# Key search and gates of a product-key layer, queued on VectorE behind the low parts of their own pair of blocks

## The chip, the cores and the metric

The kernel runs on one core of a Trainium2 chip. The metric is the time of one execution on the device in microseconds (us); of several runs the median is given. A profile is one execution, recorded by the hardware profiler; its span reaches from the first to the last instruction.

## The reference

Two transformer blocks on 256 tokens of width 1024, in float32. The first has two layers (stick-breaking attention and retention as mixers, each followed by a mixture of experts), the second runs a state space branch beside a sparse attention, and then a layer of 16384 experts that are picked by product keys. The change lies in that last layer:

```python
def peer_ffn(x, w_q, sub_k1, sub_k2, u_tab, v_tab):
    ...
    s1 = jnp.einsum('bshd,hnd->bshn', q[..., 0, :], sub_k1.astype(f32))
    s2 = jnp.einsum('bshd,hnd->bshn', q[..., 1, :], sub_k2.astype(f32))
    v1, i1 = lax.top_k(s1, PEER_TOPK)
    v2, i2 = lax.top_k(s2, PEER_TOPK)
    cand_s = (v1[..., :, None] + v2[..., None, :]).reshape(...)
    top_s, pos = lax.top_k(cand_s, PEER_TOPK)
    experts = jnp.take_along_axis(cand_i, pos, axis=-1)
    gates = jax.nn.softmax(top_s, axis=-1)
    ...
        act = jax.nn.gelu(jnp.einsum('ced,cd->ce', u, xc.astype(f32))) * gc
        return jnp.einsum('ce,ced->cd', act, v_tab[ec].astype(f32))
```

Each token has 8 heads; a head scores 128 keys of each of two halves, takes the 16 best of both, and of their 256 sums the 16 best. That gives 128 experts a token, each with a gate.

## The kernel before

The kernel does not gather experts. It computes U times every token for all 16384 experts, in a pass over 128 blocks of U (128 experts, 1024 wide, 512 KB each), keeps the result in `big` (key 2 on partitions, key 1, token), multiplies it by gates, which are zero for experts that a token did not pick, and then makes a second pass over 128 blocks of V.

**The pass over U** (`peer`, L1467) takes the blocks in pairs. SP loads a block (L1478, tile `raw`, three buffers). ScalarE rounds it to float32r (L1480, the cast, tile `pair`, three buffers). What the rounding left, the low part, is subtracted in two shares at L1483: VectorE takes three of the eight chunks (UD = 3), GpSimd the other five. TensorE then does 24 matmuls for the block (L162, `ps<-hn,pair`). After a pair ScalarE applies the gelu (L1489 for tokens whose gates are there already, L1492 for the others), and VectorE multiplies the former by their gates (L1490).

**The side work** is a generator, `select` (L1365), that yields pieces with a cost. For each half t of the tokens it searches the keys, head by head, and then runs `gates` (L1427). A head's search is L1382 to L1406: the best 16 of both score rows by MAX8, FIND_INDEX8 and MATCH_REPLACE8 (L1382, L1383, L1385, four, four and two a head), the 256 sums (L1389), their best 16 (L1393 to L1396), the places decoded (L1397 to L1399), and the keys looked up with a one-hot (L1403 on VectorE, L1405 on GpSimd, L1406 on VectorE). The softmax over the gates follows once for a half (L1409 to L1414, the exponential on ScalarE at L1410), and a transposition on TensorE (L186). `gates` then works in groups of four tokens: VectorE builds one-hots (L1440 to L1443, tile `s`), TensorE multiplies them (L162, `y<-s`, eight matmuls a group), and the result goes into `big`: where blocks of U have come, VectorE multiplies (L1454), for the others ScalarE copies (L1456).

`spend` (L114) emits pieces until their cost has used up what a call gives: 4.16 after each head of the scores before the pass, PACE = 2.81 after each pair of blocks in it. A head's search costs 5.5 in four pieces, a group of gates 1.8.

```python
    def spend(self, more):
        self.credit += more
        while self.credit > 0 and self.side:
            self.credit -= next(self.side, 1e9)
```

**What sets the order.** Each engine executes its instructions in one fixed order. A scheduler makes it when the program is built: it steps through a modelled time, and at each step gives an engine the instruction that was emitted earliest among those that are ready in that model. Pieces of the search read the scores alone, which are there before the pass begins; so nothing but the place of emission ties them to a pair of blocks. In the order before, the search of the second half stands on VectorE between blocks 9 and 42 of the pass, among the gates of the first half, though its pieces are emitted after pairs from block 52 on.

Of the kernel before, what the change touches and what calls it, by code (L numbers as in the profile page):

```python
# [50 lines left out]
# the order in which the pieces of the state space branch, of the attention and of the gates are emitted  # L51
# [3 lines left out]
class Net:  # L55
# [49 lines left out]
    def background(self, n=1):  # L105
        """emits n pieces of the work that has only to be done some time"""
        while n and self.jobs:
            try:
                next(self.jobs[0])
                n -= 1  # L110
            except StopIteration:
                self.jobs.pop(0)

    def spend(self, more):  # L114
        """emits pieces of the work of self.side, which yields what each costs, at `more` a call"""
# [31 lines left out]
    def split(self, hi, lo, src, eng=None):  # L147
        """hi = src in float32r, lo = the rest; eng, in short pieces, for lo"""
# [22 lines left out]
    def warm(self, src, n=1):  # L171
        """products that nobody reads, once src is there: they keep the clock of the tensor engine up while it waits"""
# [32 lines left out]
    def ada_rows(self, i, j, slot, out):  # L205
        """silu(c) @ w of a third (shift, scale, gate): rows 32c.. of out hold columns 256c.. of the third"""
# [22 lines left out]
    def ada_all(self, i, j, first):  # L229
        """emits in pieces; leaves self.mod[i, j] = scale, shift columns and gate rows"""  # L230
# [8 lines left out]
    def ada_cols(self, m, g_b, i, j):  # L239
        """scale and shift as columns [P, KB], folded with the last norm's g and b"""  # L240
# [24 lines left out]
    def gate_row(self, m2):  # L265
        """1 + gate on every partition [P, D]"""
# [9 lines left out]
    def row(self, cols):  # L276
        """columns [P, KB] as a row of D on every partition"""
# [10 lines left out]
    def ln_rows(self, i, j):  # L288
        """what the norm after a sublayer needs: 1 + gate, g and b on every partition"""
# [13 lines left out]
    def layer_norm(self, x, y, i, j):  # L303
        """x: residual [P, T, D], replaced by the new one; y: psum tiles y[t][half]; returns xhat"""
# [36 lines left out]
    def transposed(self, src, each, scales=None):  # L341
        """src [P, T, D], or its rows times the diagonals of scales -> each(k, psum [P, S]) for the KB blocks of D"""
# [1452 lines left out]
```

## Time and profile before

| | |
|---|---|
| median of 3 runs | 2150.25 us (2148.62 to 2151.22) |
| span of the profiled execution | 2146.3 us; its time outside the span is not recorded |
| TensorE (PE) busy | 1998.3 us, 93% |
| VectorE (DVE) busy | 1244.3 us, 58% |
| ScalarE (ACT) busy | 787.7 us, 37% |
| GpSimd (POOL) busy | 489.9 us, 23% |
| pass over U on TensorE | 1316 to 1782 us |

The profile gives a span and busy times within it; a run's time also counts what lies around the span. A busy share is a mean over stages with different limits, so the pass over U is read by itself, in stretches. The granted clock (PEclk) is TensorE's, 1.00 for 2.4 GHz, 0.50 for 1.2 GHz, and values between are means over a stretch.

### The profile page before, as it was taken

How to read it: one execution, taken by the hardware profiler on the slowest of the kernel's cores; microseconds unless marked ns; L12 is line 12 of the kernel's file. 1: busy time of each engine (PE TensorE's matmuls, PEld its weight loads, DVE VectorE, ACT ScalarE, POOL GpSimd, SP SyncE). 2: the span in 40 equal slices, each digit the busy share in tenths (PEclk: the TensorE clock that was granted, in tenths of full speed). 3: DMA queues.
4: the chain of work that ended last, by engine and by line, in shares of the span. 5: the costliest groups of instructions: out<-in, count | busy, mean ns of one | idle time of the engine just before them, and what ended most of it. 6: DMA issues, size and time to landing. Idle time of an engine off the chain costs nothing.

```text
span 2146.3 us, 32368 instructions
## 1 busy us (share of the span) xinstructions
PE 1998.3 (93%) x12822; PEld 1567.6 (73%) x12823; DVE 1244.3 (58%) x2474; ACT 787.7 (37%) x1224; POOL 489.9 (23%) x349
## 2 busy tenths in 40 slices
PE   6999999969999899997877999988999999999998
PEld 4967544428998744545765889888999998888886
DVE  4555111146885411115798569999627995565565
ACT  3353111124454111114323543444444444444444
POOL 1002000022331200002354144544665550000000
PEclk9999999989999899998998999999999999999999
DMA  9797799985875699994232361334454445555554
GB/s 389 287 398 275 286 395 394 392 317 213 297 277 171 235 387 391 395 395 180 109 106 90 123 234 40 128 119 138 165 184 158 143 148 186 188 193 188 189 192 149
DMA packets 155599, 496.11 MB, mean 231 GB/s; under 512 B 10144, under 2 KB 10560, under 8 KB 146864
## 3 DMA queue, kind: packets, MB, share of 16 engines
q1 hardware_dynamic: 152592, 483.42, 62.5%
q0 software_dynamic: 2848, 10.53, 1.3%
q8 instruction: 104, 1.70, 0.3%
q14 instruction: 55, 0.45, 0.1%
HBM read 486.30 MB, written 7.61 MB: 230 GB/s over the span
## 4 chain that ended last, share of the span: by engine, by line
PE 47%; DVE 14%; issue 2%; ACT 1%; POOL 1%; POOLq 0%; ACTq 0%; DVEq 0%
PE ps L162 25%; PE y L162 21%; DVE pair L1483 1%; DVE t L1134 1%; DVE hl L152 1%; DVE et L1406 1%; DVE i L1383 1%; DVE s L1440 1%; DVE t L1135 1%; DVE pos L1394 0%; DVE s L1442 0%; DVE v L1382 0%; POOL hl L159 0%; DVE t L1129 0%; DVE t L1130 0%
## 5 line engine op out<-in xcount | busy, mean ns | idle before, releaser
L162 PE MATMUL ps<-hn,pair 128*128 128x256 f32 x3072 | 394.8, 289 | 6.5 <-DVE pair L1483 6.5
L162 PEld LDWEIGHTS ps<-hn,pair 128*128 128x128 f32 x3072 | 382.5, 195 | 7.6 <-DVE pair L1483 7.5
L1483 POOL TENSOR_TENSOR pair<-raw,pair 128x640 fp32r<-128x640 f32 x128 | 241.7, 1892 | 183.6 <-ACT pair L1480 161.8
L162 PE MATMUL ps<-w,t 128*64 128x512 f32 x576 | 256.0, 598 | 10.6 <-ACT t L734 4.1
L162 PE MATMUL ps<-hl,t 128*64 128x512 f32 x576 | 255.6, 599 | 0.0
L150 ACT CAST hl<-w 128x2048 fp32r<-128x2048 f32 x79 | 150.1, 1903 | 146.5 <-PE ps L162 80.5
L152 DVE TENSOR_TENSOR pair<-raw,pair 128x1024 fp32r<-128x1024 f32 x128 | 156.8, 1225 | 67.2 <-ACT pair L150 67.2
L162 PE MATMUL y<-pair,tmp 128*128 128x512 f32 x768 | 189.5, 396 | 0.0
L162 PE MATMUL y<-pair,eT 128*128 128x512 f32 x768 | 186.3, 392 | 0.0
L162 PEld LDWEIGHTS y<-pair,tmp 128*128 128x128 f32 x768 | 144.7, 188 | 33.6
L162 PEld LDWEIGHTS y<-pair,eT 128*128 128x128 f32 x768 | 144.3, 188 | 32.2
L162 PEld LDWEIGHTS ps<-w,t 128*64 128x64 f32 x576 | 76.8, 137 | 124.5 <-issue 112.3
L152 DVE TENSOR_TENSOR hl<-w,hl 128x2048 fp32r<-128x2048 f32 x54 | 127.4, 2361 | 55.5 <-ACT hl L150 52.0
L1480 ACT CAST pair<-raw 128x1024 fp32r<-128x1024 f32 x128 | 134.5, 1053 | 50.7 <-PE ps L162 43.0
L159 POOL TENSOR_TENSOR hl<-w,hl 128x512 fp32r<-128x512 f32 x52 | 75.7, 1486 | 301.5 <-ACT hl L150 297.3
L688 DVE TENSOR_TENSOR t<-t,ps 128x512 f32<-128x512 f32 x16 | 11.0, 687 | 213.4 <-PE ps L162 213.4
L150 ACT CAST pair<-raw 128x1024 fp32r<-128x1024 f32 x128 | 133.8, 1045 | 1.1 <-issue 1.1
L162 PE MATMUL ps<-hl,a 128*128 128x256 f32 x1008 | 130.3, 287 | 1.8 <-ACT hl L150 1.8
L162 PEld LDWEIGHTS ps<-hl,a 128*128 128x128 f32 x1008 | 124.0, 191 | 6.1 <-issue 2.1
L1483 DVE TENSOR_TENSOR pair<-raw,pair 128x384 fp32r<-128x384 f32 x128 | 91.3, 715 | 43.5 <-ACT pair L1480 43.5
L162 PEld LDWEIGHTS ps<-a,hl 128*128 128x128 f32 x864 | 106.3, 195 | 4.2 <-issue 2.9
L162 PE MATMUL ps<-a,hl 128*128 128x256 f32 x864 | 108.5, 288 | 0.7 <-DVE a L152 0.5
(422 smaller groups left out, 3067.3 us busy)
## 6 DMA issues: line engine op xcount, KB each, us to landing
raw<-peer_u SPq DMA_DIRECT2D x128, 512.0 KB, 3.4
raw<-peer_v SPq DMA_DIRECT2D x128, 512.0 KB, 4.2
w<-ada_w SPq DMA_DIRECT2D x35, 1024.0 KB, 8.7
w<-moe_w_gate SPq DMA_DIRECT2D x24, 1024.0 KB, 16.0
w<-moe_w_up SPq DMA_DIRECT2D x24, 1024.0 KB, 14.1
w<-moe_w_down SPq DMA_DIRECT2D x24, 1024.0 KB, 14.1
hl<-moe_w_gate SPq DMA_DIRECT2D x24, 1024.0 KB, 14.3
hl<-moe_w_up SPq DMA_DIRECT2D x24, 1024.0 KB, 14.2
```

Of the source, the lines that this page charges most:

```text
L150: nc.scalar.copy(hi, src)
L152: nc.vector.tensor_tensor(lo, src, hi.bitcast(F32), op=OP.subtract)
L159: eng.tensor_tensor(lo[:, q], src[:, q], hi.bitcast(F32)[:, q], op=OP.subtract)
L162: self.nc.tensor.matmul(out, lhsT=lhsT, rhs=rhs, start=start, stop=stop, skip_group_check=True)
L688: nc.vector.tensor_tensor(hid, hid, pu, op=OP.mult)
L1134: V.tensor_tensor_scan(w[:, ri], d, a[:, ri], 0.0, op0=OP.mult, op1=OP.add)
L1135: V.tensor_tensor(a, w, bc(c), op=OP.mult)
L1383: V.max_index(ix[:, a, rs], v[:, a, rs], s)
L1406: V.tensor_reduce(et[:, 0:2, h], oh.rearrange("p a k j -> p a j k"), axis=AX.X, op=OP.add)
L1440: V.tensor_tensor(ol, self.iota4, of(0), op=OP.is_equal)
L1480: nc.scalar.copy(up[:, 0], ur)
L1483: eng.tensor_tensor(up[:, 1, ks], ur[:, ks], up[:, 0, ks].bitcast(F32), op=OP.subtract)
```

## The change

`issue_after(ins)` adds to each instruction that its block emits on the engine of `ins` an edge behind `ins`, in the order alone: no semaphore, no wait. `at` is VectorE's share of the low part of the pair's second block. So the pieces that `spend` emits after a pair stand on VectorE behind that low part. Instructions of the pieces on other engines get no edge. The test for an empty share went too (both shares are nonempty), and comments were dropped, with their lines kept; from L1483 on lines shift by one, and the low part's own line is L1482 in the changed kernel.

```diff
                 for eng, ks in ((V, slice(0, UD)), (nc.gpsimd, slice(UD, KB))):
-                    if ks.start < ks.stop:
-                        eng.tensor_tensor(up[:, 1, ks], ur[:, ks], up[:, 0, ks].bitcast(F32), op=OP.subtract)
+                    lo = eng.tensor_tensor(up[:, 1, ks], ur[:, ks], up[:, 0, ks].bitcast(F32), op=OP.subtract)
+                    at = lo if eng is V else at
...
             self.ready = i + 2
-            self.spend(PACE)
+            with self.tc.issue_after(at.ins):
+                self.spend(PACE)
```

What becomes of the order, at three places. Names in the rows: `pair` is the block's tile with its low part, `raw` the block as loaded; `s<-c_iota` and `s<-s,eT` are one-hots of the gates; `v`, `i`, `pos`, `cand`, `fi`, `oh`, `et` belong to the search.

VectorE in the pass over U, from the low part of block 26 to that of block 27 in the kernel before:

```order
L1483 TENSOR_TENSOR pair<-raw,pair 128x384
L1394 MAX_INDEX pos<-top,cand 128x8
L1454 TENSOR_TENSOR big<-y,big 128x4x24
L1490 TENSOR_TENSOR big<-s,big 128x2x40
L1440 TENSOR_TENSOR s<-c_iota_9783,eT 128x512
L1443 TENSOR_TENSOR s<-c_iota_9783,eT 128x512
L1442 TENSOR_TENSOR s<-s,eT 128x512
L1406 TENSOR_REDUCE et<-oh 128x2x16
L1387 CAST fi<-i_13294 128x32
L1396 MATCH_REPLACE cand<-top,cand 128x256
L1441 TENSOR_TENSOR s<-s,eT 128x512
L1483 TENSOR_TENSOR pair<-raw,pair 128x384
```

and, in the changed kernel, from the low part of block 25 to that of block 27, a whole pair:

```order
L1482 TENSOR_TENSOR pair<-raw,pair 128x384
L1490 TENSOR_TENSOR big<-s,big 128x2x40
L1440 TENSOR_TENSOR s<-c_iota_9783,eT 128x512
L1443 TENSOR_TENSOR s<-c_iota_9783,eT 128x512
L1454 TENSOR_TENSOR big<-y,big 128x4x24
L1441 TENSOR_TENSOR s<-s,eT 128x512
L1482 TENSOR_TENSOR pair<-raw,pair 128x384
L1442 TENSOR_TENSOR s<-s,eT 128x512
L1482 TENSOR_TENSOR pair<-raw,pair 128x384
```

The search (L1394, L1406, L1387, L1396) has left this place; a pair now has its two low parts, one product L1490, and gates alone.

VectorE further on, from block 59 to block 64, where the order before has this and nothing else:

```order
L1483 TENSOR_TENSOR pair<-raw,pair 128x384 x2
L1490 TENSOR_TENSOR big<-tmp,big 128x2x128
L1483 TENSOR_TENSOR pair<-raw,pair 128x384 x2
L1490 TENSOR_TENSOR big<-s,big 128x2x128
L1483 TENSOR_TENSOR pair<-raw,pair 128x384 x2
```

In the changed kernel, from the low part of block 61 to just ahead of that of block 62:

```order
L1482 TENSOR_TENSOR pair<-raw,pair 128x384
L1394 MAX_INDEX pos<-top,cand 128x8
L1382 MAX v_13136<-s 128x8
L1397 TENSOR_SCALAR pos<-pos 128x16
L1398 TENSOR_SCALAR pos<-pos 128x16
L1383 MAX_INDEX i_13137<-v_13136,s 128x8
L1399 CAST fi<-pos 128x32
L1385 MATCH_REPLACE s<-v_13136,s 128x128
L1403 TENSOR_TENSOR oh<-c_iota_9784,fi 128x512
L1382 MAX v_13136<-s 128x8
L1490 TENSOR_TENSOR big<-s,big 128x2x128
L1383 MAX_INDEX i_13137<-v_13136,s 128x8
```

Half a head's search now stands between two low parts here, and the rest of the head within four blocks; the eight heads of the second half take blocks 53 to 83.

ScalarE at blocks 82 and 83, before:

```order
L1480 CAST pair<-raw 128x1024 x2
L1489 ACTIVATE tmp<-ps 128x2x128
L1492 ACTIVATE big<-ps 128x2x128
L1480 CAST pair<-raw 128x1024 x2
L1489 ACTIVATE s<-ps 128x2x128
L1492 ACTIVATE big<-ps 128x2x128
L1480 CAST pair<-raw 128x1024 x2
```

and in the changed kernel:

```order
L1480 CAST pair<-raw 128x1024 x2
L1410 ACT_TABLE_LOAD
L1410 ACTIVATE et<-et 128x128
L1489 ACT_TABLE_LOAD
L1489 ACTIVATE s<-ps 128x2x128
L1492 ACTIVATE big<-ps 128x2x128
L1480 CAST pair<-raw 128x1024 x2
```

The exponential of the second half's softmax with its two table loads came from block 41 to just ahead of the cast of block 82. GpSimd's L1405 moved with the search, one to four low parts, and the load of the residual that GpSimd issues moved from ahead of its low part of block 38 to that of block 80. SP's order is unchanged, and so is VectorE's from block 86 on.

## Rows read from the trace of the kernel before

**Rows 1.** the page: span and busy time of engines (us, share of the span, instructions).
```profile
span 2146.3 us, 32368 instructions
...
PE 1998.3 (93%) x12822; PEld 1567.6 (73%) x12823; DVE 1244.3 (58%) x2474; ACT 787.7 (37%) x1224; POOL 489.9 (23%) x349
```

**Rows 2.** the page: busy tenths in 40 slices of the span, 53.7 us each.
```profile
PE   6999999969999899997877999988999999999998
...
DVE  4555111146885411115798569999627995565565
```

**Rows 3.** windows of stretches that begin at blocks 3, 12, 42, 52, 84 of U.
```profile
core 0: us, PE busy (x) PEld busy (x) DVE busy (x) ACT busy (x) POOL busy (x), PEclk, DMA share, GB/s
1325.60:1361.15 35.55, 31.17 (x238) 30.69 (x236) 35.33 (x114) 15.92 (x19) 20.73 (x14) 0.90 0.47 148
1361.15:1496.97 135.82, 116.90 (x907) 112.29 (x905) 134.35 (x376) 57.88 (x83) 61.51 (x39) 0.95 0.36 121
1496.97:1532.42 35.45, 35.45 (x299) 35.11 (x297) 31.73 (x53) 18.75 (x31) 19.16 (x11) 1.00 0.48 162
1532.42:1624.97 92.55, 92.55 (x774) 92.55 (x772) 29.02 (x56) 42.30 (x63) 61.56 (x32) 1.00 0.54 177
1624.97:1782.40 157.43, 157.43 (x1315) 155.53 (x1314) 137.60 (x226) 68.27 (x121) 84.76 (x43) 1.00 0.46 151
```

**Rows 4.** waits of TensorE, blocks 12 to 41: total us, times, longest.
```profile
PE y L162 <- DVE s L1442: 9.5, 10, 1.8
PE y L162 <- DVE s L1441: 6.6, 7, 1.5
PE ps L162 <- DVE pair L1483: 2.8, 4, 2.1
```

**Rows 5.** waits of ScalarE, the same stretch.
```profile
ACT big L1456 <- DVE big L1454: 63.7, 21, 6.9
```

**Rows 6.** waits of TensorE, blocks 3 to 11.
```profile
PE ps L162 <- DVE pair L1483: 3.6, 1, 3.6
PE y L186 <- DVE et L1406: 0.7, 1, 0.7
```

**Rows 7.** windows of VectorE (us, busy, clock, DMA), search beside low parts.
```profile
1316.00:1346.00 30.00, 29.71 (x122) 0.89 0.29 91
```

**Rows 8.** groups of instructions on VectorE, 1316 to 1346 us.
```profile
L1483 DVE TENSOR_TENSOR pair<-raw,pair 128x384 fp32r<-128x384 f32 x6 | 4.4, 735 | 0.2 <-ACT pair L1480 0.2
...
L1382 DVE MAX8 v<-s 128x8 f32<-128x128 f32 x14 | 3.5, 275 | 0.0
```

**Rows 9.** groups on VectorE and GpSimd, blocks 52 to 83.
```profile
L1483 DVE TENSOR_TENSOR pair<-raw,pair 128x384 fp32r<-128x384 f32 x31 | 17.3, 558 | 39.2 <-ACT pair L1480 39.2
...
L1490 DVE TENSOR_TENSOR big<-tmp,big 128x256 f32<-128x256 f32 x8 | 3.4, 424 | 11.3 <-ACT tmp L1489 11.3
...
L1483 POOL TENSOR_TENSOR pair<-raw,pair 128x640 fp32r<-128x640 f32 x32 | 61.7, 1929 | 31.4 <-ACT pair L1480 31.4
```

**Rows 10.** timeline of VectorE, L1397 twice: start, us taken.
```profile
1342.06 0.15 DVE L1397 TENSOR_SCALAR pos<-pos 128x16 uint32<-128x16 uint32 x1
...
1430.94 1.57 DVE L1397 TENSOR_SCALAR pos<-pos 128x16 uint32<-128x16 uint32 x1
```

**Rows 11.** the instructions of L1405 on GpSimd: duration min/median/max in ns.
```profile
L1405 POOL TENSOR_TENSOR oh<-oh,fi x16: 1047/1052/1639, 1289.9 to 1487.5; 128x512 f16<-128x512 f16 x16
```

**Rows 12.** timeline of ScalarE around the softmax of the first half.
```profile
1342.54 1.28 ACT L1410 ACT_TABLE_LOAD   x1
1343.83 0.31 ACT L1410 ACTIVATE et<-et 128x128 f32<-128x128 f32 x1
...
1345.10 1.28 ACT L1492 ACT_TABLE_LOAD   x1
```

**Rows 13.** the page: the costliest groups, the cast of a block of U.
```profile
L1480 ACT CAST pair<-raw 128x1024 fp32r<-128x1024 f32 x128 | 134.5, 1053 | 50.7 <-PE ps L162 43.0
```

## The prediction

> **What bounds the kernel now.** I read the busy times first: TensorE works in 93% of the span, VectorE in 58% [rows 1]. So TensorE sets the time, and anything that makes it wait counts. Next the slices [rows 2], each 53.7 us: TensorE falls to 7 and 8 in slices 25 to 28 (1288 to 1502 us), just where VectorE stands at 9 four times running; then VectorE drops to 6 and 2 while TensorE is at 9. The same engine is too full and then nearly empty, within one pass over U.
>
> I then cut this pass by blocks of U, at the starts of blocks 3, 12, 42, 52 and 84 on TensorE [rows 3]. In the fourth stretch (blocks 52 to 83) TensorE never waits: 774 matmuls in 92.55 us, 0.1196 us each. That is the floor. At it, the second stretch (blocks 12 to 41) would need 907 x 0.1196 = 108.5 us; it takes 135.8, so 27.3 us are lost. The first loses 35.55 - 238 x 0.1196 = 7.1 us. The third (299 matmuls) and the fifth (1315) come out within 0.4 us of the floor. VectorE is busy for 134.35 of 135.82 us in the second stretch and for 29.02 of 92.55 in the fourth.
>
> What ends TensorE's waits in the second stretch [rows 4]: 16.1 us for one-hots of the gates (L1441, L1442), 2.8 for low parts. Those one-hots are cheap; they are late since key search for the second half of the tokens, which depends on no block of U, stands among them on VectorE. Idle adds up to 18.9 us; the other 8.4 of the 27.3 are matmuls that run at a lower granted clock after the gaps (0.95 in this stretch, 1.00 in the three behind it).
>
> **The change, part by part.** No arithmetic, tile or transfer is added; only the order differs. In the changed order blocks 12 to 51 have gates and low parts alone on VectorE, the eight heads of search for the second half stand in blocks 53 to 83, and from block 86 on VectorE's order is the old one.
>
> 1. *Blocks 12 to 41, search gone.* The nearest row is the third stretch of the old kernel: blocks 42 to 51, the same gates of the first half with low parts and no search, in nearly the order that blocks 12 to 41 now get. It runs at the floor, at 31.73 us of VectorE in 35.45 [rows 3]. What ScalarE does there is a little different: it copies the part of the gates whose block has not come yet, and that part is larger early on. Those copies now wait for L1454 on VectorE (63.7 us in 21 waits [rows 5]), with the casts of U queued behind them; L1454 is held up by the same full queue. I take all but 0.3 of the 27.3 back: **-27**. If the copies alone held up a quarter of it, -20; more than -27.3 cannot come from here.
>
> 2. *Blocks 3 to 11.* The first block of the pass finds a backlog of search on VectorE (3.6 us of waiting [rows 6]). That order is unchanged up to the low part of block 3, so this stays. The later wait of 0.7 us for the end of the first half's search (L186 on L1406) goes, since pieces of the second half no longer stand before it; with the slow clock behind it **-1** (bounds: 0, and -3 if low parts that come sooner also catch up some of the rest).
>
> 3. *Blocks 52 to 83, search arrives.* This is what the change pays. In 1316 to 1346 us VectorE does search and low parts only: 29.71 us busy [rows 7], of which 4.4 are six low parts, and 14 of L1382, of which a head has four: 3.5 heads [rows 8]. So a head takes (29.71 - 4.4) / 3.5 = 7.2 us. Two pairs of blocks, which the new order gives to each head, add four low parts and two products L1490: at their quiet durations 4 x 0.56 + 2 x 0.42 [rows 9] the sum is 10.3 us, with low parts at the 0.735 of [rows 8] it is 11.0. TensorE takes 92.55 / 8 = 11.57 us for the four blocks. So the search just fits, with 0.6 to 1.3 us to spare. The cover is thin, because VectorE also waits for GpSimd: L1397 takes 0.15 us alone and 1.57 while GpSimd works [rows 10]. GpSimd is busy for 20.73 of 35.55 us (58%) where I measured the head [rows 3]; in blocks 52 to 83 it will have 61.56 + 8 x 1.05 (L1405 [rows 11]) of 92.55, 76%. One more full wait a head (1.42) gives 12.4 us, and 8 x (12.4 - 11.57) = 6.8. Some of this is absorbed: with three buffers TensorE has two blocks ahead of it, 5.8 us, of which the cast takes 1.05 [rows 13] and GpSimd's part 1.93 [rows 9], leaving about 2.5. So the stretch costs 0 without further waits, 4.3 with one a head, and 15.6 with two (13.8 us a head). Half a wait more is nearest to the step from 58 to 76%; I take **+2.5**, the slower clock after idling included.
>
> 4. *Block 82, the switch to gates.* The softmax of the second half now falls right before it is needed. ScalarE loads a table, takes the exponential and loads the table back, 1.28 + 0.31 + 1.28 = 2.9 us [rows 12], between two casts of U, in a stretch that had no such break. GpSimd idles 31.4 us over 32 low parts there [rows 9], 1 us each, so part is hidden. Between 0 and 2.9: **+1**.
>
> The sum is -27 - 1 + 2.5 + 1 = -24.5 us. The profiled execution has a span of 2146.3 [rows 1], 4 us below the median of the runs, 2150.25, which counts what lies around the span; I expect a span near 2122 and a time of **2126 us**. Hidden and costed at nothing: the one transfer that moves from before GpSimd's low part of block 38 to that of block 80 (the residual for the end, needed some 200 us later), and SP's loads, whose order is unchanged.
>
> **A rule that speaks against this change.** A full wait of L1397 behind GpSimd is what [rows 10] show. The Trainium skill, "SBUF — State Buffer", section "Who interferes with whom", says more: VectorE instructions with two SBUF inputs, or in a two-port mode, and GpSimd instructions hold one port pair in turn, each for its whole length. By that rule alone the four GpSimd parts, L1405, the four low parts and the two products would already fill 4 x 1.93 + 1.05 + 4 x 0.56 + 2 x 0.42 = 11.9 us of the 11.57, before the search's own contending instructions: rival one below, about 2139 us.
>
> **Rivals.**
> *One: the search stretch becomes bound by VectorE.* Two further waits a head, 13.8 us, cost 15.6: 2150.25 - 28 + 15.6 + 1 = 2139 us (2133 to 2144). For it: 76% of GpSimd. Against: the fifth stretch runs VectorE 137.6 of 157.4 us beside GpSimd with no loss [rows 3]. Chance 0.17.
> *Two: slower than before.* The same place, but low parts, search and GpSimd block each other in turn, each low part waiting behind search that waits for GpSimd. It decides from the point where the 28 us gained and the 2.5 of slack are spent: 30.5 / 8 = 3.8 us over 11.57, so 15.4 us a head, four to five full waits above 10.3 or 11.0. At 16 us, 8 x 4.43 - 2.5 = 33, and 2156 us. Nothing in the old profile shows VectorE that slow; chance 0.05.
> *Three: no change.* TensorE's waits in blocks 12 to 41 come from the gates' own loop (one-hots, products, L1454, copy, cast), and last. For it: 63.7 us of waits on ScalarE [rows 5]. Against: the third and fifth stretch have the same loop and no loss. 2146 to 2154; chance 0.09.
> The forecast, 2118 to 2133, has the remaining 0.69.
>
> **How the numbers follow.** 0.2% of the time is 4.3 us, about what a measurement here can tell from no change. Forecast and rival one lie below 2145.9: faster 0.86. Rival three is same, 0.09; rival two slower, 0.05. The lower end takes the best of each term, 2150.25 - 27.3 - 3 = 2120, and 2 us for what they leave out: 2118. The upper end takes rival one and most of item 4, or item 1 at -20 with the rest as forecast: 2141. For rivals two and three and the far tail of rival one, 0.2 is left out.
>
> **What would show it.** In the new profile blocks 12 to 41 should take 109 us at a clock of 1.00, without waits for L1441 and L1442; VectorE should be near 9 tenths or more in blocks 52 to 83, where any wait of TensorE should be for low parts (L1482) and be below 5 us; blocks 84 on should take 157 us as before. Waits for one-hots that stay in blocks 12 to 41 would make rival three right; waits above 10 us for low parts in blocks 52 to 83, rival one.

## The result, and the profile after

The changed kernel takes **2123.18 us** (median of 4 runs, 2122.27 to 2127.13); beside them, the kernel before took 2149.43 (4 runs, 2146.96 to 2151.22). The ratio is 0.9886, with a 95% interval of 0.987 to 0.9903. The forecast was 2126, in a range of 2118 to 2141.

From the page of the changed kernel, the first lines and the busy tenths of two engines [rows 1, 2]:

```profile
span 2120.5 us, 32377 instructions
...
PE 1990.3 (94%) x12820; PEld 1560.4 (74%) x12823; DVE 1243.6 (59%) x2474; ACT 791.2 (37%) x1224; POOL 483.3 (23%) x349
...
PE   6999999988999999997887999999999999999998
...
DVE  4555111137895411114598668867999995555555
```

VectorE does the same work (1243.6 us busy, 1244.3 before), but its full slices have moved: the four 9s that stood at 1288 to 1502 us are gone, five now stand in slices 29 to 33 (1484 to 1749 us, slices of 53.0), the first three of them from the search that has come there, and TensorE is at 9 from slice 23 to the last but one.

The same five stretches of the pass over U as in [rows 3], by the starts of blocks 3, 12, 42, 52 and 84:

```profile
core 0: us, PE busy (x) PEld busy (x) DVE busy (x) ACT busy (x) POOL busy (x), PEclk, DMA share, GB/s
1326.17:1359.56 33.39, 30.01 (x237) 29.53 (x236) 30.91 (x80) 15.88 (x19) 20.31 (x14) 0.95 0.51 159
1359.56:1467.66 108.10, 108.10 (x907) 107.16 (x905) 74.76 (x164) 59.02 (x84) 52.79 (x30) 1.00 0.44 147
1467.66:1503.10 35.44, 35.44 (x300) 35.10 (x297) 28.11 (x73) 18.19 (x28) 17.22 (x10) 1.00 0.46 150
1503.10:1599.53 96.43, 93.34 (x775) 92.74 (x772) 93.37 (x280) 45.20 (x66) 65.93 (x41) 1.00 0.58 181
1599.53:1756.90 157.37, 157.37 (x1315) 155.49 (x1314) 141.04 (x228) 68.35 (x121) 85.23 (x43) 1.00 0.47 151
```

Against [rows 3] that is -2.2, **-27.7**, 0.0, **+3.9** and -0.1: -26.1, and the span fell by 25.8. In blocks 12 to 41 no wait of TensorE is left, at a granted clock of 1.00, and ScalarE's copies wait 7.6 us for L1454 in place of the 63.7 of [rows 5]; waits of ScalarE, blocks 12 to 41, after:

```profile
ACT big L1456 <- DVE big L1454: 7.6, 15, 0.6
```

What the change pays is in blocks 52 to 83. TensorE's waits there (total us, times, longest):

```profile
PE ps L162 <- DVE pair L1482: 1.8, 1, 1.8
PE y L186 <- DVE et L1406: 1.3, 1, 1.3
```

And VectorE's groups there, to be held against [rows 9] (count, then busy us and mean ns):

```profile
L1482 DVE TENSOR_TENSOR pair<-raw,pair 128x384 fp32r<-128x384 f32 x31 | 26.2, 844 | 0.6 <-ACT pair L1480 0.6
L1406 DVE TENSOR_REDUCE et<-oh 128x32 f32<-128x512 f16 x8 | 9.1, 1131 | 0.0
L1490 DVE TENSOR_TENSOR big<-tmp,big 128x256 f32<-128x256 f32 x8 | 8.9, 1113 | 0.0
...
L1397 DVE TENSOR_SCALAR pos<-pos 128x16 uint32<-128x16 uint32 x8 | 1.2, 155 | 0.0
```

A low part takes 844 ns instead of 558, a product of `tmp` 1113 instead of 424; L1397, the instruction by which the prediction priced this, takes 155 ns on average and does not wait. How it happens is in the timeline of one head, VectorE first (each row: start in us, us taken):

```profile
1541.37 1.13 DVE L1482 TENSOR_TENSOR pair<-raw,pair 128x384 fp32r<-128x384 f32 x1
1542.43 1.14 DVE L1406 TENSOR_REDUCE et<-oh 128x32 f32<-128x512 f16 x1
1543.48 0.88 DVE L1482 TENSOR_TENSOR pair<-raw,pair 128x384 fp32r<-128x384 f32 x1
...
1545.99 1.61 DVE L1490 TENSOR_TENSOR big<-tmp,big 128x256 f32<-128x256 f32 x1
```

and GpSimd in the same 7 us:

```profile
1540.73 1.36 POOL L1405 TENSOR_TENSOR oh<-oh,fi 128x512 f16<-128x512 f16 x1 [2.23 <-DVE oh L1403]
1542.05 5.27 POOL L1482 TENSOR_TENSOR pair<-raw,pair 128x640 fp32r<-128x640 f32 x3
```

GpSimd idles 2.23 us for L1403, then works without a break until 1547.3. VectorE's two subtractions and its product, which read two tiles, end only after one of GpSimd's instructions has ended; the reduction and the searches between them are not held. Such waits are some 2.1 us of this head (1.13, 0.88 and 1.61 against 0.54, 0.54 and 0.41).

Which of the two engines starts first decides who is held. In the kernel before the same two shares of a low part also run side by side, block after block, but there VectorE idles when the cast ends and starts 0.05 us ahead:

```profile
1540.08 0.56 DVE L1483 TENSOR_TENSOR pair<-raw,pair 128x384 fp32r<-128x384 f32 x1 [0.78 <-ACT pair L1480]
1540.13 1.95 POOL L1483 TENSOR_TENSOR pair<-raw,pair 128x640 fp32r<-128x640 f32 x1 [1.44 <-ACT pair L1480]
```

So it goes for 30 of the 31 low parts that VectorE starts in blocks 52 to 83. VectorE takes its 0.56 us, and it is GpSimd's share that is longer (1.94 us; 1.57 where nothing is beside it, as further down in onehot_on_vector). In the change 23 of the 31 low parts on VectorE start while one of GpSimd's instructions runs, and each of them ends 0.41 to 0.43 us after that instruction; the other eight take 0.56 us or less.

The low part of block 52 on VectorE ends 3.4 us before TensorE starts on that block, the low part of block 60 only 0.9. From there on the low parts of blocks 64, 68, 72 and 76 start 11.79 us apart, and TensorE needs 11.52 for four blocks: the lead shrinks by 0.27 us a head, to 0.05 at block 76. So TensorE stops only near the end, at block 80 for a low part and at L186 for the last head.

### The profile page after: what moved, and what is told of

Read it like the earlier page. It is cut to its first block, busy times and chain, and to the rows that moved or that the text cites. A ratio compares the mean times of both kernels' runs of the same rounds, so it can differ in the third digit from the quotient of the medians.

```text
span 2120.5 us, 32377 instructions
## 1 busy us (share of the span) xinstructions
PE 1990.3 (94%) x12820; PEld 1560.4 (74%) x12823; DVE 1243.6 (59%) x2474; ACT 791.2 (37%) x1224; POOL 483.3 (23%) x349
## 4 chain that ended last, share of the span: by engine, by line
PE 73%; DVE 11%; issue 2%; ACT 2%; POOL 1%; POOLq 0%; DVEq 0%; ACTq 0%
PE ps L162 46%; PE y L162 26%; DVE t L1134 1%; DVE hl L152 1%; DVE pair L1482 1%; PE ps L186 1%; DVE hl L159 1%; DVE et L1406 1%; DVE t L1135 1%; DVE i L1383 0%; POOL hl L159 0%; DVE t L1129 0%; DVE t L1130 0%; PE y L1140 0%; DVE pos L1394 0%
## 5 line engine op out<-in xcount | busy, mean ns | idle before, releaser
L162 PE MATMUL ps<-hn,pair 128*128 128x256 f32 x3072 | 384.2, 285 | 4.3 <-DVE pair L1482 4.3
L162 PEld LDWEIGHTS ps<-hn,pair 128*128 128x128 f32 x3072 | 375.1, 192 | 5.0 <-DVE pair L1482 4.9
L1482 POOL TENSOR_TENSOR pair<-raw,pair 128x640 fp32r<-128x640 f32 x128 | 234.5, 1838 | 161.0 <-ACT pair L1480 154.5
L162 PE MATMUL ps<-w,t 128*64 128x512 f32 x576 | 257.7, 601 | 11.4 <-ACT t L734 5.8
L162 PE MATMUL ps<-hl,t 128*64 128x512 f32 x576 | 257.3, 601 | 0.0
L162 PE MATMUL y<-pair,tmp 128*128 128x512 f32 x768 | 189.5, 395 | 0.0
L162 PE MATMUL y<-pair,eT 128*128 128x512 f32 x768 | 186.3, 391 | 0.0
L162 PEld LDWEIGHTS ps<-w,t 128*64 128x64 f32 x576 | 77.2, 138 | 126.5 <-issue 116.0
L162 PEld LDWEIGHTS y<-pair,tmp 128*128 128x128 f32 x768 | 144.3, 188 | 33.9
L162 PEld LDWEIGHTS y<-pair,eT 128*128 128x128 f32 x768 | 144.1, 188 | 32.5
L162 PE MATMUL ps<-hl,a 128*128 128x256 f32 x1008 | 130.2, 287 | 1.8 <-ACT hl L150 1.8
L162 PEld LDWEIGHTS ps<-hl,a 128*128 128x128 f32 x1008 | 124.0, 191 | 6.1 <-issue 2.1
L162 PEld LDWEIGHTS ps<-a,hl 128*128 128x128 f32 x864 | 106.5, 195 | 4.1 <-issue 2.9
L162 PE MATMUL ps<-a,hl 128*128 128x256 f32 x864 | 108.7, 287 | 0.5 <-DVE a L152 0.4
L162 PEld LDWEIGHTS ps<-hl,t 128*64 128x64 f32 x576 | 76.7, 138 | 41.8 <-issue 41.3
```

Source lines behind the costliest of these rows:

```text
L162: self.nc.tensor.matmul(out, lhsT=lhsT, rhs=rhs, start=start, stop=stop, skip_group_check=True)
L1482: lo = eng.tensor_tensor(up[:, 1, ks], ur[:, ks], up[:, 0, ks].bitcast(F32), op=OP.subtract)
```

## The experiments

The time up to block 0 differs from run to run: block 0 starts between 1312.3 and 1322.0 us in these traces, with no pattern by kernel that one execution of each could show. The stretches inside the pass repeat to 0.1 us (blocks 12 to 41 take 108.10 us in five different kernels, 108.13 in a sixth). So each kernel is read by its stretches, named by their blocks; the last one ends here where block 127 starts. All columns but the last two are us of the one profiled execution. The ratios are to runs of the kernel before that were taken beside each kernel, and kernels are compared by them.

| kernel | 3–11 | 12–51 | 52–83 | 84–126 | median us | ratio to before, 95% |
|---|---|---|---|---|---|---|
| before | 35.5 | 171.3 | 92.6 | 154.4 | 2149.43 | |
| the change | 33.4 | 143.5 | 96.4 | 154.3 | 2123.18 | 0.9886 (0.987–0.9903) |
| edge_gates_only | 35.3 | 174.4 | 92.6 | 154.3 | 2152.03 | 1.0021 (1.0007–1.0035) |
| half_the_search_early | 35.1 | 159.7 | 95.3 | 154.3 | 2138.11 | 0.9958 (0.9942–0.9975) |
| search_low4 | 33.4 | 143.5 | 95.7 | 154.3 | 2119.43 | 0.9871 (0.9852–0.9889) |
| search_low2 | 33.4 | 143.6 | 105.1 | 154.3 | 2127.89 | 0.9909 (0.9892–0.9927) |
| onehot_on_vector | 33.4 | 143.5 | 109.2 | 154.3 | 2137.55 | 0.994 (0.9916–0.9963) |
| search_paced | 33.4 | 143.6 | 102.6 | 154.4 | 2127.3 | 0.9889 (0.9867–0.9911) |
| less_search_ahead | 26.7 | 142.7 | 98.8 | 159.0 | 2129.69 | 0.9898 (0.9873–0.9922) |
| all_three | 26.7 | 145.4 | 103.1 | 161.1 | 2140.9 | 0.9962 (0.9947–0.9977) |
| product_on_gpsimd | 33.4 | 143.5 | 105.4 | 155.8 | 2132.26 | 0.9903 (0.9887–0.992) |
| less_ahead_paced | 26.6 | 149.4 | 103.3 | 154.3 | 2126.24 | 0.9876 (0.9856–0.9896) |
| low_on_scalar | 33.4 | 143.5 | 92.6 | 154.3 | 2121.41 | 0.986 (0.9842–0.9878) |
| less_ahead_later_pace | 26.6 | 145.5 | 95.2 | 154.3 | 2116.88 | 0.9849 (0.9836–0.9863) |

### Is the gain the search that left blocks 12 to 41?

The changed kernel holds both kinds of pieces behind their pair. *edge_gates_only* holds the gates alone and sets the search free (`EDGE_GATES` is true, and `gating` is true ahead of each piece of the gates):

```diff
-    def spend(self, more):
+    def spend(self, more, at=None):
...
         while self.credit > 0 and self.side:
-            self.credit -= next(self.side, 1e9)
+            if at is not None and self.gating == EDGE_GATES:
+                with self.tc.issue_after(at):
+                    self.credit -= next(self.side, 1e9)
+            else:
+                self.credit -= next(self.side, 1e9)
```

> The edge behind the low part is kept for the pieces of the gates and dropped for those of the search. Crowding theory (search of the second half among the gates of the first is the cause): all is as before the change, blocks 12 to 41 take about 135 us with waits of TensorE for one-hots, blocks 52 to 83 take 92.6, time 2146 to 2152. Rival (the gates' own loop is the cause, and the edge mends it): blocks 12 to 41 take 109 us, time 2119 to 2125.

*half_the_search_early* holds everything but four of the eight heads of the second half (the same code, with a flag that is set for those heads).

> The first four heads of the second half's search get no edge and go back among the gates, the other four stay late. Crowding theory: about half of the 27.7 us are lost again in blocks 12 to 41 (118 to 126 us there, the waits at its beginning), blocks 52 to 83 lose their 3.9 us extra; time 2130 to 2140. Rival (the gates' own loop): the loss does not go with the number of heads, 2123 or 2149.

Blocks 12 to 41 of edge_gates_only by the windows, and below one of TensorE's waits there (L168 is this kernel's L162, L1448 its L1441):

```profile
1357.36:1494.94 137.58, 115.94 (x908) 110.28 (x905) 135.88 (x385) 57.54 (x83) 63.97 (x39) 0.97 0.35 123
```

```profile
PE y L168 <- DVE s L1448: 10.2, 7, 2.2
```

and the stretch in half_the_search_early:

```profile
1356.77:1481.02 124.25, 113.37 (x907) 110.79 (x905) 104.05 (x259) 57.46 (x84) 58.34 (x35) 0.96 0.38 131
```

With the search free, VectorE is full again (135.88 of 137.58 us), the waits for one-hots are back and the time is that of the kernel before, even slightly above it. With half of the search there, blocks 12 to 41 take 124.25 us: 11.6 of the 27.7 us are gained. Its expectation missed in blocks 52 to 83: with four heads left there they still take 95.3 us, 2.7 above the kernel before, where none of the 3.9 us was to be left. The gates' loop is the same in all of these, so the search among the gates is the cause, and rival three is out.

### What lengthens blocks 52 to 83?

The first idea was the balance of the low part between the two engines. *search_low4* and *search_low2* give VectorE four or two chunks in place of three, in blocks 52 to 83 (search_low2 has 2 for 4):

```diff
-for eng, ks in ((V, slice(0, UD)), (nc.gpsimd, slice(UD, KB))):
+for eng, ks in ((V, slice(0, 4 if 52 <= i < 84 else UD)), (nc.gpsimd, slice(4 if 52 <= i < 84 else UD, KB))):
```

> In blocks 52 to 83 alone VectorE takes four of the eight chunks of a low part, GpSimd four (three and five in the changed kernel, where a head takes 11.79 us on VectorE and TensorE needs 11.52 for its four blocks). Theory (VectorE waits for GpSimd): a head loses about 1.2 us of GpSimd and gains 0.6 on VectorE and falls to 11.0 to 11.5 us; blocks 52 to 83 in 93 to 95 us instead of 96.4, time 2119 to 2122. Rival (VectorE's own work is the bound): a head takes about 12.4 us, the stretch 99 to 102, time 2126 to 2130.

> In blocks 52 to 83 alone VectorE takes two of the eight chunks, GpSimd six. Theory (VectorE waits for GpSimd): GpSimd gains 1.2 us a head, VectorE loses 0.6; a head takes 12.2 to 12.8 us, the stretch 99 to 106, time 2126 to 2133. Rival (VectorE's own work is the bound): a head falls to about 11.2 us and the stretch to 93 to 94, time 2119 to 2121.

search_low2, with less arithmetic on VectorE, is worse by 8.6 us in the stretch, as the theory of waits for GpSimd had it and not its rival. Its windows row, and in its groups VectorE's low part, which is a third narrower and takes 1141 ns in place of 844:

```profile
1500.48:1605.54 105.06, 96.35 (x774) 94.49 (x772) 98.35 (x281) 45.17 (x66) 71.28 (x41) 0.98 0.48 166
```

```profile
L1482 DVE TENSOR_TENSOR pair<-raw,pair 128x256 fp32r<-128x256 f32 (+1 forms) x31 | 34.8, 1141 | 0.0
```

search_low4 came out at a time within what its theory gave, but for the larger part by an earlier block 0 (1313.5 against 1316.8); its stretch is only 0.75 us shorter (95.68) and misses the 93 to 95 us of that theory. There the low parts of blocks 64 and 76 start 35.88 us apart, 11.96 a head, no faster than in the change.

Then five kernels tried to give VectorE air. *onehot_on_vector* takes L1405 of the second half off GpSimd, so that no low part waits behind it:

```diff
-nc.gpsimd.tensor_tensor(oh, oh, fi[:, 1, :, :, None]..., op=OP.mult)
+(V if t else nc.gpsimd).tensor_tensor(oh, oh, fi[:, 1, :, :, None]..., op=OP.mult)
```

> L1405, the product of the key one-hots, goes from GpSimd to VectorE in the second half's search. In the changed kernel GpSimd stands still for 2.2 us a head ahead of it, waiting for L1403 with a low part queued behind. Queue theory: without it GpSimd takes its low parts as soon as the casts end, VectorE pays 0.3 to 0.5 us a head and gets back most of 2.1 us of waiting: a head takes 10.8 to 11.4 us, blocks 52 to 83 93 to 94.5 us, time 2118 to 2122. Rival (VectorE's own work): a head takes 12.1 to 12.3 us, the stretch 99 to 100, time 2125 to 2128.

*search_paced* spreads the second half's search (its costs times 1.08) and makes up for it with cheaper gates of the first half (1.69 for 1.8):

> The pieces of the second half's search cost 8% more and groups of gates of the first half 0.11 less, so that a head is given 4.2 blocks (12.2 us) and the gates of the first half, where VectorE is busy for 75 of 108 us, come a little denser. Theory (a head needs 11.79 us and is paced at 11.3, so that it lags until the buffers are used up at block 79): no lag, no wait for a low part; blocks 52 to 83 in 93 to 95 us, blocks 12 to 51 as much longer or shorter as they hold more or fewer gates, time 2119 to 2122. Rival (the waits at blocks 79 and 81 come from the softmax and the transposition there, not from lag): they stay, 2123 to 2125.

*less_search_ahead* lowers SCORE from 4.16 to 3.5, so that less search stands on VectorE when the pass begins:

> The budget of search a head of the scores before the pass is 3.5 instead of 4.16, so some 5 of cost move from before the pass into it, where each piece has its low part ahead. Theory (the 5.6 us lost in blocks 3 to 8 are VectorE's backlog of search at the start of the pass): blocks 3 to 11 take 28.5 to 31 us instead of 33.4, time 2118 to 2122. Rival (the backlog is set by when the scores come, not by the budget): no change, 2122 to 2125; if the gates then end after the last block, up to 2130.

*all_three* has these three edits together:

> The three edits before together. If the three losses (backlog at the start, lag of the search, wait at its end) are separate, they add: 33.4 to 30 us in blocks 3 to 11, 96.4 to 93 in blocks 52 to 83, time 2114 to 2119. If the later search pushes the last gates past the last block of U, the pass over V starts late and the time is 2120 to 2128.

*product_on_gpsimd* moves L1490 of blocks 52 to 83 onto GpSimd:

```diff
-V.tensor_tensor(big[:, i:i + 2, :n], tmp, big[:, i:i + 2, :n], op=OP.mult)
+(nc.gpsimd if 52 <= i < 84 else V).tensor_tensor(big[:, i:i + 2, :n], tmp, big[:, i:i + 2, :n], op=OP.mult)
```

> The changed kernel, with the products of L1490 of blocks 52 to 83 on GpSimd in place of VectorE; nothing else differs. In the changed kernel VectorE takes 11.79 us for a head's search with two pairs of blocks (its low parts of blocks 64, 68, 72, 76 start 11.79 us apart), TensorE 11.52, and blocks 52 to 83 take 96.43 us instead of 92.55. Theory: VectorE's two-input instructions (L1482, L1490) wait for whole GpSimd instructions; of a head's time 0.41 + 1.61 us are the two products. Without them a head takes 9.8 to 10.5 us, less than TensorE's, so blocks 52 to 83 take 92.6 to 94.5 us (the wait at L186, 1.3 us, stays), and the time is 2119 to 2122 us. Rival: GpSimd's own queue sets the stretch: a head then gives it 8.3 us of work, two products of some 0.65 us (by width, from the low part's 1.57 for 640 columns) and 2.2 us of waiting for L1403, 11.8 us; low parts come late, blocks 52 to 83 take 97 us or more, 2124 to 2130 us.

None of the five shortened the stretch, and none was faster than the change; onehot_on_vector and all_three came out slower than even their rivals gave. less_search_ahead has 793 matmuls in the stretch, 18 more than the change, which at 0.1196 us each are 2.15 of its 2.40 us more; its other stretches are looked at further down. In search_paced a head takes 2.1 pairs, so its pieces meet other blocks each time; its low parts are hardly shorter (822 ns), and the products of `s`, 410 ns in the change, take 1309. all_three takes 103.1 us in the stretch, less than onehot_on_vector alone, and loses again behind it, as less_search_ahead does: 161.1 us for blocks 84 to 126, and 374.8 from block 127 on, where the change takes 366.7. In onehot_on_vector the stretch is 109.17 us, though GpSimd idles more. VectorE over one head of it:

```profile
1567.35 1.35 DVE L1482 TENSOR_TENSOR pair<-raw,pair 128x384 fp32r<-128x384 f32 x1
...
1571.45 1.73 DVE L1482 TENSOR_TENSOR pair<-raw,pair 128x384 fp32r<-128x384 f32 x1
...
1574.49 1.67 DVE L1482 TENSOR_TENSOR pair<-raw,pair 128x384 fp32r<-128x384 f32 x1
...
1578.01 1.77 DVE L1490 TENSOR_TENSOR big<-s,big 128x256 f32<-128x256 f32 x1
1579.71 0.68 DVE L1405 TENSOR_TENSOR oh<-oh,fi 128x512 f16<-128x512 f16 x1
```

and GpSimd, four low parts, each started just ahead of one of those:

```profile
1566.71 1.57 POOL L1482 TENSOR_TENSOR pair<-raw,pair 128x640 fp32r<-128x640 f32 x1 [1.60 <-ACT pair L1480]
1571.20 1.56 POOL L1482 TENSOR_TENSOR pair<-raw,pair 128x640 fp32r<-128x640 f32 x1 [2.92 <-ACT pair L1480]
1574.17 1.57 POOL L1482 TENSOR_TENSOR pair<-raw,pair 128x640 fp32r<-128x640 f32 x1 [1.40 <-ACT pair L1480]
1577.94 1.57 POOL L1482 TENSOR_TENSOR pair<-raw,pair 128x640 fp32r<-128x640 f32 x1 [2.20 <-ACT pair L1480]
```

Four of VectorE's instructions now wait for half of a low part or more (4.5 us beyond their 0.54 and 0.41) where the change had three, 2.1 us. In the change GpSimd is late, its low parts run back to back, and most of that run lies beside MAX8, FIND_INDEX8 and the reduction, which do not wait. Without L1405 ahead of them GpSimd stands idle when a cast ends and starts its low part at once. VectorE is still in a search then, comes to its next two-input instruction 0.07 to 0.64 us later, and is held. In the kernel before it was the other way round: VectorE was there first. product_on_gpsimd shows the same loss: VectorE has two instructions fewer per head, and is busy for longer (98.11 us of 105.40; 93.37 of 96.43 in the change). On VectorE, one pair of low parts of it:

```profile
1559.37 3.38 DVE L1482 TENSOR_TENSOR pair<-raw,pair 128x384 fp32r<-128x384 f32 x2
```

The rival in its expectation, GpSimd's own queue, has the direction, but not the place: the waits of TensorE in the stretch (10.0 us, 11 times) are all for VectorE's low part.

### The direct test

If VectorE waits for GpSimd's low parts, then without them the stretch must be free. *low_on_scalar* lets ScalarE, which has room there, fill those five chunks with a copy of the block. It leaves out their subtraction, so it is a test and no version to use:

```diff
+if eng is not V and 52 <= i < 84:
+    nc.scalar.copy(up[:, 1, ks], ur[:, ks])
+    continue
 lo = eng.tensor_tensor(up[:, 1, ks], ur[:, ks], up[:, 0, ks].bitcast(F32), op=OP.subtract)
```

> The changed kernel, but in blocks 52 to 83 the five chunks of the low part that GpSimd makes are filled by ScalarE, which copies the block there (it leaves out the subtraction for them); GpSimd keeps only L1405 in that stretch. It costs ScalarE some 0.7 us a block (128x640 by the cast's 1.05 for 128x1024), 22 us on top of its 45 of 96. Theory: the stretch is long because VectorE's two-input instructions wait for GpSimd's low parts; in the changed kernel they take 18.1 us there beyond their shortest durations (L1482 9.3, L1490 5.7, others 3), 2.3 a head, and the more of it a kernel of this study has, the longer its stretch (search_low4 16.4 and 95.7 us, search_paced 24.1 and 102.6, search_low2 27.5 and 105.1). Then without those low parts the excess falls below 3 us, a head takes 9.5 to 10.2 us in place of 11.79, and blocks 52 to 83 take 92.6 to 94.3 us, of which up to 1.7 is the wait at L186; the time is 2118 to 2121 us. Rival: the excess is VectorE's own (an instruction that waits for the one before it, or for a semaphore that the profile does not show); it then stays above 10 us and the stretch above 95.5, 2122 or more.

Blocks 52 to 83 of it by the windows, and below VectorE's low part and product in its groups (lines shift by three):

```profile
1508.32:1600.88 92.56, 92.56 (x775) 92.56 (x773) 78.50 (x273) 63.80 (x96) 13.74 (x11) 1.00 0.58 188
```

```profile
L1485 DVE TENSOR_TENSOR pair<-raw,pair 128x384 fp32r<-128x384 f32 x31 | 18.6, 599 | 10.3 <-ACT pair L1480 10.3
...
L1493 DVE TENSOR_TENSOR big<-tmp,big 128x256 f32<-128x256 f32 x8 | 3.3, 407 | 0.0
```

92.56 us is the stretch of the kernel before [rows 3], to 0.01 us. VectorE executes the same search and the same share of the low part in 78.50 us instead of 93.37 (273 and 280 instructions fall into the windows): of the 14.9 us that its busy time in the change is longer, 13.2 are waits in the low parts (31 x 245 ns = 7.6) and the products (8 x 706 ns = 5.6). The median, 2121.41, lies 0.4 above what was expected, with the stretch in place: block 0 starts at 1322.0 us in its profiled execution. One thing this test cannot part: it also takes GpSimd's share off the way of the block, and so may have the five chunks ready sooner. But TensorE's waits in the change were for VectorE, not for GpSimd.

### A better version

less_search_ahead showed one true gain: blocks 3 to 11 run without a backlog. And it showed where that was lost. Its windows rows for blocks 3 to 11 and 84 to 126, and below the longest wait of TensorE behind the start of block 127:

```profile
1327.71:1354.36 26.65, 26.38 (x221) 26.18 (x220) 25.08 (x72) 14.89 (x19) 17.91 (x13) 1.00 0.49 174
...
1595.90:1754.87 158.97, 155.78 (x1275) 152.69 (x1276) 151.79 (x240) 66.04 (x119) 86.91 (x43) 0.99 0.43 147
```

```profile
PE y L162 <- DVE eT L152: 3.4, 1, 3.4
```

The side work behind comes later by some blocks, so the last gates stand at the end of the pass (240 of their 256 matmuls came before block 127), and the pass over V waits for them: from block 127 on it takes 373.8 us, 366.7 in the change, and 3.4 of these 7.1 us are the wait shown. *less_ahead_paced* makes the cost good with a higher pace before block 52, *less_ahead_later_pace* only from block 20 on:

```diff
-SCORE = 4.16
+SCORE = 3.5
...
-                self.spend(PACE)
+                self.spend(3.14 if 20 <= i < 52 else PACE)   # less_ahead_paced: 3.0 if i < 52
```

> The changed kernel with less search before the pass (3.5 in place of 4.16 after each head of the scores) and a pace of 3.0 instead of 2.81 after pairs before block 52, so that the second half's search and gates end where they end in the changed kernel. With less search ahead alone, blocks 3 to 11 took 26.65 us instead of 33.39, but the rest of the pass and the V pass gave back 13 us. Theory: the gain is real (a backlog of search on VectorE at the start of the pass, 2.5 us of wait and a clock of 0.95), and the loss came only from gates that ended late. Then blocks 3 to 11 have a clock of 1.00, the time from block 84 on is as in the changed kernel, and the time is 2117 to 2121 us. Rival: the later start of the first half's gates crowds blocks 12 to 51 or shifts the search of the second half against the blocks, as the slower search did (102.64 us for blocks 52 to 83): 2123 to 2131 us.

> The changed kernel with less search before the pass (3.5 for 4.16 after each head of the scores), and a pace of 3.14 instead of 2.81 after the pairs of blocks 20 to 51 alone: the whole cost emitted by block 52 is then the same as in the changed kernel, so that the second half's search meets the same blocks (GpSimd's order from block 53 on is the same), and the first half's gates still start one group at a time. In less_ahead_paced blocks 3 to 11 took 26.6 us, but block 14, where two groups of gates came at once, cost 3.9 us, and blocks 52 to 83 took 103.3 as the search met the blocks elsewhere. Theory (the place where search meets low parts decides, to one piece): blocks 3 to 11 take 26.6, blocks 12 to 51 145.2 to 146 (40 x 24 + 256 = 1216 matmuls at 0.1196), blocks 52 to 83 96.4, from 84 on 154.3 as in the changed kernel; the pass is 4 to 5 us shorter than in the changed kernel, 2117 to 2120 us. Rival: what comes before shifts VectorE against GpSimd in the search stretch even with the same order; blocks 52 to 83 then take 99 us or more, 2121 to 2127 us.

The first failed, by its rival: two groups of gates came at once at block 14, and the search met the blocks elsewhere. Its heads up to block 71 are slow (low parts of blocks 64 and 68 start 14.64 us apart), and from block 72, where its pattern is that of the change, 11.79. The second has GpSimd's order of the change from block 53 on:

```profile
1329.81:1356.43 26.62, 26.38 (x221) 26.18 (x220) 25.05 (x72) 14.86 (x19) 17.89 (x13) 1.00 0.53 174
1356.43:1465.53 109.10, 109.10 (x915) 108.17 (x914) 79.36 (x171) 58.63 (x83) 54.70 (x32) 1.00 0.46 150
1465.53:1501.90 36.37, 36.37 (x307) 36.01 (x305) 29.34 (x78) 18.83 (x29) 17.26 (x10) 1.00 0.44 145
1501.90:1597.13 95.23, 93.42 (x775) 92.81 (x772) 92.20 (x281) 45.27 (x66) 66.23 (x41) 1.00 0.57 183
```

From block 0 to block 127 it takes 431.04 us, the change 437.05, the kernel before 463.05. At 2116.88 us (5 runs, 2116.12 to 2120.23) it beats both, and its interval of the ratio lies below that of the change.

Blocks 52 to 83 were to take 96.4 us, as in the change, and take 95.23. Those 1.2 us are luck of the profiled execution: they are lost or won ahead of block 80, where two starts moved against each other by less than 0.1 us. GpSimd's low part and VectorE's there, in the change:

```profile
1584.10 1.53 POOL L1482 TENSOR_TENSOR pair<-raw,pair 128x640 fp32r<-128x640 f32 x1 [0.18 <-ACT pair L1480]
1584.22 1.82 DVE L1482 TENSOR_TENSOR pair<-raw,pair 128x384 fp32r<-128x384 f32 x1
```

and in less_ahead_later_pace:

```profile
1583.07 2.00 POOL L1482 TENSOR_TENSOR pair<-raw,pair 128x640 fp32r<-128x640 f32 x1 [0.27 <-ACT pair L1480]
1583.11 0.53 DVE L1482 TENSOR_TENSOR pair<-raw,pair 128x384 fp32r<-128x384 f32 x1
```

With GpSimd 0.12 us ahead VectorE's share is held, with 0.04 us it is not, and GpSimd's is the longer one. TensorE waits 1.8 us for a low part in the change and 0.5 here.

## Why the prediction was right

**Item 1, blocks 12 to 41: -27, measured -27.7.** Shown by edge_gates_only and half_the_search_early. The stretch went to the floor with a clock of 1.00, and the copies on ScalarE did not hold it up (7.6 us of waits, 0.6 the longest). It passed the bound of 27.3 by 0.4, since the floor was taken from blocks without gates: 0.1196 us a matmul, where this stretch needs 108.10 / 907 = 0.1192. One reading on the way was wrong: in slices 25 to 28 of [rows 2] TensorE is at 9, 9, 8 and 8, and its 7s stand in slices 19, 21 and 22, ahead of the pass. Nothing rests on it, since [rows 3] measures the stretch.

**Item 2, blocks 3 to 11: -1, measured -2.1.** Within its bounds, but the working was wrong in part. "This stays" was said of the first wait, 3.6 us; it is 2.5 now, because the low part of block 4 takes 0.53 us and not 1.68. The later wait for L1406 (0.7), which was to go, is still there, 0.9. That most of the stretch's loss is a backlog of search from ahead of the pass is shown by less_search_ahead: 26.65 us for nine blocks of 24 matmuls, 25.8 at the floor.

**Item 3, blocks 52 to 83, search arrives: +2.5, measured +2.4 up to the start of block 81.** The mechanism was right, VectorE in waits for GpSimd. The size agrees by luck, since two errors cancel. The prediction took half a wait a head, 11.7 us (11.0 and half of 1.42). By its own formula that costs nothing, since 8 x 0.14 = 1.1 us is less than its 2.5 of slack; the +2.5 was chosen between 0 and the 4.3 for one wait a head. Measured is nearer to one wait a head. VectorE's low part of block 52 ends at 1499.69 us and that of block 80 at 1586.04: seven heads, 12.3 us each on average, where one full wait made 12.4. The low parts of blocks 56 and 60 start 13.85 us apart, the four heads behind them take 11.79 each. And the slack is larger, the 3.4 us of VectorE's lead at block 52 (the prediction's own terms, 5.8 - 1.05 - 1.93, make 2.8). Who waits was wrong too. "L1397 takes 0.15 us alone and 1.57 while GpSimd works" was the price, but L1397 takes 155 ns here, and the waits sit in the low parts and the products.

**Item 4, block 82: +1, measured +1.5 from block 81 to 83.** TensorE waits 1.3 us for L1406 there. The chain behind it, in the change:

```profile
1588.53 0.31 ACT L1410 ACTIVATE et<-et 128x128 f32<-128x128 f32 x1 [3.20 <-DVE et L1409]
...
1588.86 1.28 ACT L1489 ACT_TABLE_LOAD   x1
...
1590.57 0.43 DVE L1490 TENSOR_TENSOR big<-s,big 128x256 f32<-128x256 f32 x1 [0.96 <-ACT s L1489]
...
1591.78 0.56 DVE L1482 TENSOR_TENSOR pair<-raw,pair 128x384 fp32r<-128x384 f32 x1 [0.58 <-ACT pair L1480]
```

L1406 stands right behind this low part of block 82, and VectorE idles 0.96 and 0.58 us ahead of it for ScalarE, which has its second table load, the gelus and the cast in between. So the loads are in the chain, as predicted. But the exponential was itself late, by 3.20 us of ScalarE's waiting for L1409, the softmax's first step, which stands behind a search that lags; the prediction had no such term. In low_on_scalar the same loads stand at the same block and VectorE idles the same 0.96 and 0.58 us, but its search does not lag, and TensorE does not wait there: blocks 81 and 82 take what they took before. The loads cost only what the lag has left uncovered; how the 1.5 us divide between the two was not tried.

**Rivals.** One, a stretch bound by VectorE at 13.8 us a head, did not come with this change, but it was near: onehot_on_vector takes 109.17 / 8 = 13.6 us a head and 2137.55 us, where rival one had 2139. Two, slower than before from 15.4 us a head on, was not reached by any kernel on the average of its heads; 15.4 is three to four full waits above 10.3 or 11.0 (4.4 or 5.1 us at 1.42 each), not the four to five that the prediction counts. The signs named for rival one hold: waits for low parts, 1.8 us in the change, 12.3 in onehot_on_vector.

**Who holds up whom.** That VectorE's two-input instructions wait for whole instructions of GpSimd was the prediction's reason to fear this stretch, and the timelines above show it, with one condition: GpSimd's has started first. The Trainium skill, "SBUF — State Buffer", section "Who interferes with whom", says that a VectorE instruction with two SBUF inputs contends with a GpSimd instruction that reads SBUF, and that on this chip a reduction never does. The traces agree: L1406 takes 1131 ns on average beside GpSimd's runs in the change, 1130 in onehot_on_vector and 1118 in low_on_scalar, while the low parts go from 599 (low_on_scalar) to 844 and 933. By that rule alone the prediction added up 11.9 us a head, which was to be rival one, 2139 us. That many heads take 11.79 us is no proof of the sum: in onehot_on_vector GpSimd does less, and a head takes 13.6. A sum of durations does not give it; which of two instructions starts first does.

**Open.** Why block 0 starts up to 10 us earlier or later was not tried. The load of the residual, costed at nothing, holds GpSimd just ahead of its low part of block 80, for 0.59 us of waiting and 0.57 to issue it; the reason given, that its data are needed 200 us later, says nothing of GpSimd's queue, and whether it adds to TensorE's wait at block 80 was not tried. Nor was a kernel that computes the low parts of blocks 52 to 83 without GpSimd; that would show what the remaining 2.7 us of the better version are worth.

## What to carry to other kernels

Independent work that a scheduler brings forward to an engine with a full queue delays everything that is due there; tie it to a place where that engine idles, and check in the stretch it came from and in the one it goes to that the engine fits under the bound. Where VectorE and GpSimd share a job in step, do not only add up their busy times, but look in the timeline which of two neighbouring instructions starts first: VectorE that stood ready lost nothing beside GpSimd here, and VectorE that came 0.1 us behind it was held until GpSimd's instruction had ended. So moving one instruction off either engine may make both slower. When a pace of side work is changed, keep the total emitted by the next stage the same, or the next stage meets its work elsewhere.

## What was not expected of the hardware

Taking L1405 (1293 ns on average) from GpSimd cost 1.6 us a head, (109.17 - 96.43) / 8, of which its own time on VectorE is 0.68 where it does not wait. Narrowing VectorE's low part from 384 to 256 columns, with GpSimd's at 768 in place of 640, made it longer, 1141 ns for 844. A cast of 128x32 that takes 0.17 us (L1387) took 1.95 once, at 1582.03 us in the change, and ended with a low part of GpSimd; it stands two instructions ahead of the low part for which TensorE waits 1.8 us at block 80.
